# Sample queries and keys projected beside the out-projection of the layer before; turned prompt rows copied by ScalarE and stored, with value rows, from ScalarE's queue

## The chip, the cores and the metric

The kernel runs on one core of one Trainium2 chip. The metric is the device time of one execution in microseconds; the time given for a kernel is the median of its runs.

## What is computed

One inference step of four layers over 1024 prompt rows and 32 sample rows (8 sequences of 4 tokens), width 1024, fp32. Layers 0 and 3 mix with a gated short convolution, layer 1 with a gated linear recurrence (RG-LRU), layer 2 with differential attention. A layer modulates its input, mixes, projects out, adds the residual and normalises. What the change touches is the end of layer 1 and the start of layer 2:

```python
xp = layer_norm(DEEPNORM_ALPHA * xp + gtp * op, ln_g[i], ln_b[i])   # op = mixer output @ w_out
xs = layer_norm(DEEPNORM_ALPHA * xs + gts * osm, ln_g[i], ln_b[i])
...
q, k, v, z = jnp.split(u @ w_in, [QK_WIDTH, 2 * QK_WIDTH, 2 * QK_WIDTH + V_WIDTH], axis=-1)
q = rope_partial(q.reshape(bsz, t, 2 * N_HEADS, HEAD_DIM), pos) * (HEAD_DIM ** -0.5)
k = rope_partial(k.reshape(bsz, t, 2 * N_HEADS, HEAD_DIM), pos)
...
s_past = jnp.einsum('bqhd,bkhd->bhqk', q, k_past)     # sample queries against 2048 cached keys
```

Prompt queries attend to prompt keys; sample queries attend to 16 cached pages per sequence, found through a page table, and to their own new keys. Rotated keys and values of both groups are also outputs.

## The kernel before, in words

Prompt and sample columns stand side by side: 1056 columns in three chunks of 384, 384 and 288, the last holding 256 prompt and the 32 sample columns. Every large product is made of three fp32r products (high and low parts), so one 128-row output block of one chunk takes 24 instructions of TensorE (`gemm_chunk`, line 120).

**Between layers** `boundary` (line 1618) runs `out_proj` (line 264): chunk by chunk, 8 output blocks each. In the first chunk the eight weights are loaded (`ld`, through two `raw` slots of 512 KB and a split by ScalarE and DVE). For each block it loads a residual tile xr from SP's queue (two buffers), multiplies, and adds on DVE (line 287). After a chunk, `norm` turns it (rt), normalises, and `modulate` (line 227) turns it back (xt) and writes the next layer's input units, `us` holding the sample columns for layer 2 (line 260). The chunks run in the order 0, 1, 2.

**Layer 2** starts with `qkv` (line 985): the weights stand in six column groups n of 512 (two each of q, k, v), each loaded in four parts through the same two `raw` slots and split (lines 1003, 1004). `prompt_tile` (line 1053) makes 128 prompt rows of one group: 24 products (line 1060), a scaled copy by ScalarE (1064), for q and k a rotation on DVE (1016 to 1027), four transposes into a single PSUM bank (1073), a copy of it by DVE (qkfs, 1075), and a store to qd or kd from SP's queue (1076). Value rows are stored from SP too (1069, 1085). The sample rows of groups 0 to 3 are made in tiles 1 to 4 of group 0: the four weight parts of a group are fetched again unsplit (`fetch(..., "s")`), `sample_half` (1007) multiplies with column tiling (four 32-column strips of the array), and `sample_rows` (1031) copies, sums the strips with a selection matrix `sel`, rotates and transposes into qsb and ksb. Those of groups 4 and 5 use the weights when they pass for the prompt.

**Beside** `qkv` and the gate projection `zpath` runs the key stream of the samples, `sample_keys`: pages of 256 KB fetched from GpSimd's queue (1354) into a ring of six, turned by DVE (1444), multiplied in bursts (1388), then softmax and turning. It needs qsb and ksb. `attn_layer` (line 1529) weaves the two: `merge` hands out side steps in proportion to the main work's cost, and three prompt tiles run before the first side step. When the gate projection and the key stream are emitted, `heads` (line 1138) starts: it loads keys (twice, into raw slots, then split), values V and queries of a head, and runs 64 blocks of causal attention, with the sample values (128 pages of 512 KB on SP's queue) woven in.

The order on each engine's queue is fixed when the program is built: a scheduler simulates the emitted instructions and orders them by simulated time, with tile buffers and pool memory reused through waits. At run time each queue is in order.

## Time and profile before

| | us |
|---|---|
| median of 3 runs | 2441.85 (2439.98 to 2446.5) |
| profiled execution, its own time | 2443.42 |
| its span | 2441.8 |
| TensorE busy in the span | 2297.3 (94%) |
| DVE busy | 1469.6 (60%) |
| ScalarE busy | 910.1 (37%) |
| DMA, mean rate over the span | 161 GB/s |

The profile is one execution; PE stands for TensorE, PEld for its weight load, ACT for ScalarE, POOL for GpSimd, SP for the queue of SyncE that issues most DMAs. Times in views are counted from the span's start. The out-projection of layer 1 lies at 817 to 925 us, the projections of layer 2 with the key stream at 925 to 1507 us, the heads at 1507 to 1880 us. A wait is put down to what came last; PEclk is the granted share of TensorE's full clock.

### The profile page before, as it was taken

What the parts mean: (1) busy time and instruction counts of PE and PEld (TensorE: products, weight loads), DVE (VectorE), ACT (ScalarE), POOL (GpSimd) and SP (SyncE); (2) the same over time, 40 slices, a digit from 0 to 9 for tenths busy, and PEclk for the clock granted to TensorE, in tenths of its full rate; (3) what the DMA queues carried; (4) which work ended last, traced back from release to release, by engine and by line L of the source; (5) the groups of instructions that cost most, each with busy time, mean ns of one, the idle gap of its engine ahead of it and who ended that gap; (6) DMA issues with size and microseconds to landing.
All of it is one profiled execution on the core that took longest, in us unless ns stands there. A gap on an engine that the chain in (4) does not pass through costs nothing.

```text
span 2441.8 us, 45387 instructions
## 1 busy us (share of the span) xinstructions
PE 2297.3 (94%) x17288; PEld 1952.8 (80%) x17288; DVE 1469.6 (60%) x3047; ACT 910.1 (37%) x1874; POOL 341.7 (14%) x541
## 2 busy tenths in 40 slices
PE   7999999999999998998989997889898999999997
PEld 4989999997888995466656786555566999999997
DVE  5866665467555555555654553676676477666655
ACT  4333333245555233111111111666665254333410
POOL 0200000001010001222223222333321000000000
PEclk9999999999999998999999998999999999999999
DMA  9243335334344425656768765999992321222442
GB/s 327 80 141 105 96 113 164 119 97 124 119 138 130 147 83 185 211 180 211 234 200 271 235 216 170 294 283 293 294 320 87 100 93 53 70 62 71 123 132 75
DMA packets 289392, 393.42 MB, mean 161 GB/s; under 512 B 18749, under 2 KB 197054, under 8 KB 289174
## 3 DMA queue, kind: packets, MB, share of 16 engines
q1 hardware_dynamic: 268694, 323.40, 43.3%
q0 software_dynamic: 20480, 67.13, 8.8%
q8 instruction: 136, 2.23, 0.4%
q14 instruction: 82, 0.67, 0.1%
HBM read 331.14 MB, written 59.31 MB: 160 GB/s over the span
## 4 chain that ended last, share of the span: by engine, by line
PE 67%; issue 13%; DMA 10%; POOLq 4%; DVE 2%; POOL 2%; ACT 1%; SPq 1%; DVEq 0%; ACTq 0%
PE op L127 15%; PE inX L605 12%; PE inZ L605 6%; DMA vp<-cache_v 4%; PE xb L127 4%; PE z L127 4%; PE in L127 3%; POOLq L1347 3%; PE inY L605 3%; PE ada L195 3%; DMA tok<-qd 2%; PE in L726 2%; PE in L641 2%; PE qk L1060 2%; PE zz L127 2%
## 5 line engine op out<-in xcount | busy, mean ns | idle before, releaser
L1060 PE MATMUL qk<-wq,ua 128*128 128x512 f32 x1152 | 289.6, 408 | 2.5 <-DVE wq L1004 2.5
L1060 PEld LDWEIGHTS qk<-wq,ua 128*128 128x128 f32 x1152 | 218.8, 193 | 72.1 <-issue 18.2
L1444 DVE STREAM_TRANSPOSE kt<-kp 128x512 f32<-128x512 f32 x256 | 171.3, 696 | 127.4 <-DMA kp<-cache_k 95.1
L1354 POOL DMA_DIRECT2D kp<-cache_k x256 | 140.4, 548 | 391.8 <-DVE kt L1444 262.5
L1177 PE MATMUL S<-ks,qhl 128*128 128x512 f32 (+2 forms) x384 | 109.9, 396 | 24.5 <-issue 12.3
L1229 ACT ACTIVATE P<-S,rr 128x512 f32<-128x512 f32 (+2 forms) x192 | 110.5, 581 | 49.7 <-DVE rr L1217 26.7
L287 DVE SCALAR_TENSOR_TENSOR r<-op,gate,xr 128x384 f32<-128x384 f32 (+1 forms) x96 | 54.3, 570 | 116.8 <-PE op L127 79.6
L1177 PEld LDWEIGHTS S<-ks,qhl 128*128 128x128 f32 x384 | 61.3, 198 | 60.1 <-ACT P L1229 24.6
L1492 PE MATMUL sacc<-vp,pv 128*16 128x256 f32 x1024 | 81.2, 395 | 24.1 <-DMA vp<-cache_v 23.8
L127 PEld LDWEIGHTS z<-ub,wrz 128*128 128x128 f32 x576 | 92.6, 188 | 11.7 <-issue 10.1
L127 PE MATMUL z<-ub,wrz 128*128 128x384 f32 (+1 forms) x576 | 98.2, 326 | 0.0
L1064 ACT ACTIVATE qkr<-qk 128x512 f32<-128x512 f32 x48 | 28.4, 594 | 186.1 <-PE qk L1060 146.9
L127 PEld LDWEIGHTS zz<-ua,wz 128*128 128x128 f32 x576 | 93.6, 190 | 3.6 <-issue 3.4
L127 PE MATMUL zz<-ua,wz 128*128 128x384 f32 (+1 forms) x576 | 96.1, 326 | 0.0
L1270 PEld LDWEIGHTS pv<-V,wt 128*128 128x128 f32 x576 | 75.8, 198 | 23.0 <-ACT wt L1262 11.6
L127 PEld LDWEIGHTS xb<-ub,wrx 128*128 128x128 f32 x504 | 80.9, 188 | 12.7 <-issue 9.2
L1388 PE MATMUL sps<-kt,qbd 32*32 32x512 f32 x2048 | 86.2, 625 | 4.1 <-DVE kt L1444 2.7
L1270 PE MATMUL pv<-V,wt 128*128 128x128 f32 x576 | 84.5, 289 | 4.3 <-ACT wt L1262 3.6
L324 POOL TENSOR_TENSOR rs<-mv,mhalf 128x1 f32<-128x1 f32 (+1 forms) x36 | 19.2, 540 | 494.5 <-DVE mv L322 489.0
L127 PE MATMUL xb<-ub,wrx 128*128 128x384 f32 (+1 forms) x504 | 87.8, 328 | 0.0
L195 PE MATMUL ada<-wada,ct 128*32 128x512 f32 x384 | 82.5, 616 | 4.3 <-DMA wada<-w_ada 3.1
L127 PE MATMUL op<-ub,ua 128*128 128x384 f32 (+1 forms) x504 | 85.5, 326 | 0.0
(488 smaller groups left out, 5176.0 us busy)
## 6 DMA issues: line engine op xcount, KB each, us to landing
kp<-cache_k POOLq DMA_DIRECT2D x256, 256.0 KB, 3.7
vp<-cache_v SPq DMA_DIRECT2D x128, 512.0 KB, 10.0
wada<-w_ada SPq DMA_DIRECT2D x96, 512.0 KB, 4.2
xa<-xat SPq DMA_DIRECT2D x64, 192.0 KB, 2.2
wra<-a_w_in SPq DMA_DIRECT2D x24, 512.0 KB, 4.1
wrb<-a_w_in SPq DMA_DIRECT2D x24, 512.0 KB, 4.1
xr<-xa SPq DMA_DIRECT2D x64, 192.0 KB, 2.5
tok<-kd SPq DMA_DIRECT2D x32, 256.0 KB, 9.6
```

Source lines behind the costliest of these rows:

```text
L127: nc.tensor.matmul(ps[:, :n], wt[:, wp, k], self.ucols(units[k], up, c), start=i == 0, stop=i == 3 * KB - 1)
L195: nc.tensor.matmul(ps[c : c + 32, :], self.ct[:, k], wts[k // 2][:, k % 2], start=k < 4, stop=k >= 4, tile_position=(0, c),)
L605: nc.tensor.matmul(B[tgt][jj][:, :QH], w[n][:, wp, k], mov[k](jj, up), start=new and m == 0, stop=m == 11, skip_group_check=not new)
L1060: nc.tensor.matmul(ps, u[k][:, c0 : c0 + 128], wq[n, k // 2][:, wp, k % 2], start=i == 0, stop=i == 3 * KB - 1)
L1177: nc.tensor.matmul(st[:, o : o + w], qs[h, g][:, part, s, 128 * qj : 128 * qj + 128], ks[h][:, s, l0 : l0 + w], start=part == 0, stop=part ...
L1229: nc.scalar.activation(p[:, o : o + w], x["S"][s][i][:, :w], AF.Exp, scale=-1.0, bias=rr[:, 6 + s : 7 + s], accum_out=rr[:, c : c + 1])
L1270: nc.tensor.matmul(x["pv"], x["w"][kb // 4][:, j : j + 128], V[h][:, kb], start=kb == 0, stop=kb == qb)
L1347: ld, (r,) = nc.values_load_multi_w_load_instructions(self.ptab[0:1, idx : idx + 1], engines=[et], min_val=0, max_val=159)
L1354: d = eng.dma_start(t, a[src].rearrange(pat)[bass.ds(r, 1), :, cs].rearrange("a p f -> p (a f)"))
L1388: nc.tensor.matmul(ps[b][32 * g : 32 * g + 32, r], qf[rows, f, g, k], kt[rows, g, k], start=f == 0 and k == 0, stop=f == 1 and k == 3, til ...
L1444: nc.vector.transpose(ktv[:, :, j], ring.pop(0).rearrange("p (f t) -> p f t", t=32))
L1492: nc.tensor.matmul(acc[32 * g : 32 * g + 16, :], pt[:k, j, g], vv[:k, :, g], start=j == 0, stop=j == NPG, tile_position=(0, 32 * g))
```

## The change

The sample rows of q and k (groups 0 to 3) are made in `boundary` of layer 1, by a generator `sample_qk`, one step of which is taken before each of the 16 blocks of the second and third chunk. A step fetches one weight part of 512 KB, one step ahead, and multiplies the part before it (two k blocks). The result is summed over the strips, rotated and transposed as before, with one PSUM bank ("acc", the bank Q) for both products; `out_proj` keeps three banks where it had four, and the turned tiles xat have four buffers where they had six. As the sample columns are needed early, the chunk order of that out-projection becomes 2, 0, 1, and group 0 of `qkv` starts with tiles 6 and 7. The selection matrix is made in `setup`, the rotation table and qsb, ksb stand in a pool opened before the boundary.

In `prompt_tile` ScalarE copies the turned rows (fs) and issues their store and the two stores of value rows; the store of rotated keys to the output stays on SP. The key stream is woven in after one prompt tile instead of three. `heads` loads its first keys, values and queries when 20 of the 24 steps of the gate projection are emitted, from a pool of its own; before, this came after the key stream.

`rope` becomes a method `rotate`, and `sample_rows` keeps only the value groups.

```diff
@@ -156,6 +156,11 @@
         self.mhalf = cp.tile([128, KB * NQ], F32, name="mhalf")
         nc.gpsimd.memset(self.mhalf, -0.5)
         self.us = cp.tile([128, KB, S], F32, name="us")
+
+        self.sel = cp.tile([128, 128], F32, name="sel")
+        for g in range(4):
+            nc.vector.tensor_reduce(
+                self.sel[:, 32 * g : 32 * g + 32], self.ident.rearrange("p (g j) -> p j g", g=4), axis=AX.X, op=ALU.add)
...
-    def out_proj(self, l, wout, yu, wu):
+    def out_proj(self, l, wout, yu, wu, order, hook):
...
-        for c in range(3):
+        for ci, c in enumerate(order):
             c0, n = CH[c]
             npr = min(n, T - c0)
             rt = []
             for d in range(KB):
-                if c == 0 and d + 1 < KB:
+                if ci == 0 and d + 1 < KB:
                     ld(d + 1)
+                if ci > 0:
+                    next(hook, None)
...
-                if c == 2 and d == 7:
+                if ci == 2 and d == 7:
                     yield c, rt, False
...
-            ps.append(self.half(l, c, i, rt, 1, self.mm if c == 2 and i >= 1 else self.tp))
+            ps.append(self.half(l, c, i, rt, 1, self.mm if first and i >= 1 else self.tp))
...
+    def sample_qk(self):
+        nc, a = self.nc, self.a
+        wv = a["d_w_in"][0].rearrange("(k p) f -> p k f", p=128)
+        todo = [(n, j) for n in range(4) for j in range(4)]
+        raws = []
+
+        def fetch():
+            if todo:
+                n, j = todo.pop(0)
+                raws.append(self.raw([128, 2, 512], f"wq{n}_{j}s"))
+                nc.sync.dma_start(raws[-1], wv[:, 2 * j : 2 * j + 2, 512 * n : 512 * n + 512])
+
+        def rows(n, pr):
+            kind, m = "qk"[n // 2], n % 2
+            ps = self.bank("acc", f"qss{n}")
+            nc.tensor.matmul(ps, self.sel, pr, start=True, stop=True)
+            rt = self.tmp.tile([128, 512], F32, tag="sr", bufs=1, name=f"qsr{n}")
+            nc.scalar.mul(rt, ps, -0.125 if kind == "q" else 1.0)
+            self.rotate(rt, 128, 8, self.tmp, 2)
+            if kind == "k":
+                nc.sync.dma_start(
+                    a["k_sample"][0, :, :, 8 * m : 8 * m + 8, :].rearrange("b t s f -> (b t) (s f)"), rt[:S]
+                )
+            dst = self.qsb if kind == "q" else self.ksb
+            nc.vector.transpose(dst[:, 16 * m : 16 * m + 16].rearrange("p f t -> p (f t)"), rt)
+
+        fetch()
+        done = None
+        for n in range(4):
+            if done:
+                rows(*done)
+            acc = self.bank("acc", f"qs{n}")
+            for j in range(4):
+                fetch()
+                raw = raws.pop(0)
+                for k in (2 * j, 2 * j + 1):
+                    c = 32 * (k % 4)
+                    nc.tensor.matmul(
+                        acc[c : c + 32, :], self.us[:, k], raw[:, k % 2], start=k < 4, stop=k >= 4,
+                        tile_position=(0, c))
+                yield
+            pr = self.tmp.tile([128, 512], F32, tag="spr", bufs=1, name=f"qsp{n}")
+            nc.scalar.copy(pr, acc)
+            done = n, pr
+        rows(*done)
...
         def prompt_tile(n, t):
             kind, m = "qkv"[n // 2], n % 2
...
-                rope(rt, 128, t)
+                self.rotate(rt, 128, t, self.ropep, 4)
             rows = slice(128 * t, 128 * t + 128)
             if kind == "v":
-                nc.sync.dma_start(self.vd[rows, 512 * m : 512 * m + 512], rt)
+                nc.scalar.dma_start(self.vd[rows, 512 * m : 512 * m + 512], rt)
             else:
                 ft = self.tp(f"qkf{n}_{t}")
                 for j in range(4):
                     nc.tensor.transpose(ft[:, 128 * j : 128 * j + 128], rt[:, 128 * j : 128 * j + 128], self.ident)
                 fs = self.pq.tile([128, 512], F32, tag="fs", bufs=3, name=f"qkfs{n}_{t}")
-                nc.vector.tensor_copy(fs, ft)
-                nc.sync.dma_start(
+                nc.scalar.copy(fs, ft)
+                nc.scalar.dma_start(
                     self.qkT["qk".index(kind)][512 * m : 512 * m + 512, rows].rearrange("(j p) t -> p j t", p=128),
                     fs.rearrange("p (j t) -> p j t", j=4),
                 )
@@ -1082,7 +1121,7 @@
                     a["k_prompt"][0, 0, rows, 8 * m : 8 * m + 8, :].rearrange("p s f -> p (s f)"), rt
                 )
             if kind == "v":
-                nc.sync.dma_start(
+                nc.scalar.dma_start(
                     a["v_prompt"][0, 0, rows, 4 * m : 4 * m + 4, :].rearrange("p s f -> p (s f)"), rt
                 )

@@ -1090,18 +1129,12 @@
         for j in range(4):
             load(0, j)
         for n in range(6):
-            for t in range(8):
-                d = t - 2 if n == 0 else t
+            for i in range(8):
+                d = i - 2 if n == 0 else i
                 if n < 5 and d in (0, 1, 3, 4):
                     load(n + 1, (0, 1, None, 2, 3)[d])
-                prompt_tile(n, t)
-                if n == 0 and 1 <= t < 5:
-                    for e in range(2):
-                        fetch(t - 1, 2 * e, "s")
-                        fetch(t - 1, 2 * e + 1, "s")
-                        sample_half(t - 1, e)
-                    sample_rows(t - 1)
-                if n > 3 and t == 0:
+                prompt_tile(n, (6, 7, 0, 1, 2, 3, 4, 5)[i] if n == 0 else i)
+                if n > 3 and i == 0:
...
-                ks[h] = self.pp.tile([128, 2, T], F32R, tag="ks", bufs=self.n_ks, name=f"ks{h}")
-                V[h] = self.pp.tile([128, 8, 128], F32, tag="V", bufs=2, name=f"V{h}")
+                ks[h] = self.ppa.tile([128, 2, T], F32R, tag="ks", bufs=self.n_ks, name=f"ks{h}")
+                V[h] = self.ppa.tile([128, 8, 128], F32, tag="V", bufs=2, name=f"V{h}")
...
+        keys(0, 0)
+        queries(0, 0)
+        keys(0, 1)
+        yield 0

         self.cmask = self.pp.tile([128, 512], F32, name="cmask")
         nc.gpsimd.memset(self.cmask[:, :384], 0.0)
         nc.sync.dma_start(self.cmask[:, 384:], self.a["cmask"])
-        keys(0, 0)
-        keys(0, 1)
-        queries(0, 0)
...
-        for _ in range(3):
-            next(g)
-        merge(g, 45 * 5120.0, keys, self.shares[0] * KEY_COST)
+        next(g)
+        merge(g, 47 * 5120.0, keys, self.shares[0] * KEY_COST)
         cq.__exit__(None, None, None)
         ct, self.tmp = self.pool("tmpq", reuse_waits="tile")
-        merge(self.zpath(u), 8 * 10.2 * NT, keys, self.shares[1] * KEY_COST)
+        z, ztot = self.zpath(u), 8 * 10.2 * NT
+        merge(itertools.islice(z, 20), ztot, keys, self.shares[1] * KEY_COST)
+
+        cpa, self.ppa = self.pool("ppa", reuse_waits="tile")
+        hs = self.heads(u)
+        next(hs)
+        merge(z, ztot, keys, self.shares[1] * KEY_COST)
         rest(keys)
...
-        def boundary(l, wout, y, u):
+        def boundary(l, wout, y, u, order=(0, 1, 2), hook=iter(())):
             first = None
-            for c, rt, full in self.out_proj(l, wout, y, u):
+            for c, rt, full in self.out_proj(l, wout, y, u, order, hook):
                 if not full:
+                    for _ in hook:
+                        pass
+                    self.deal(tp="PPPQ", mm="RRRU")
...
+            cs, sp = self.pool("smq", side="right")
+            self.rope = sp.tile([128, 2, 9, 16], F32, name="rope")
+            nc.sync.dma_start(self.rope, a["rope"])
+            self.qsb = sp.tile([128, 32, S], F32, name="qsb")
+            self.ksb = sp.tile([128, 32, S], F32, name="ksb")
             ct, self.tmp = self.pool("tmpm", reuse_waits="tile", side="right")
-            boundary(1, a["r_w_out"][0], A, B)
-        cms = [ct, cb]
+            self.bufs = dict(bufs, xat=4)
+            self.deal(tp="PPPU", mm="RRR", acc="Q")
+            boundary(1, a["r_w_out"][0], A, B, (2, 0, 1), self.sample_qk())
...
```

## Rows read from the trace of the kernel before

**Rows 1.** Windows: us, busy us (instructions) of PE, PEld, DVE, ACT, POOL; clock; DMA share; GB/s
```profile
817.00:925.00 108.00, 108.00 (x708) 107.05 (x707) 55.99 (x119) 34.48 (x55) 3.18 (x6) 1.00 0.36 111
925.00:1507.00 582.00, 531.67 (x4658) 385.74 (x4657) 310.63 (x650) 104.23 (x167) 145.53 (x272) 0.95 0.67 212
...
1507.00:1880.00 373.00, 312.88 (x2486) 205.29 (x2484) 250.62 (x657) 241.25 (x733) 113.28 (x80) 0.94 0.92 266
```

**Rows 2.** Waits of PE, 925 to 1510: who, for whom, total us, times, longest
```profile
PE qkf L1073 <- DVE qkfs L1075: 10.2, 5, 4.2
PE qs L1012 <- DMA wq_3s<-d_w_in: 9.6, 3, 3.9
PE spn L1397 <- DVE qkfs L1075: 7.6, 2, 5.6
...
PE qs L1012 <- DMA wq_0s<-d_w_in: 3.8, 1, 3.8
...
PE qk L1060 <- DVE wq L1004: 2.5, 2, 2.2
```

**Rows 3.** Waits of POOL, DVE, ACT and SP's queue, 925 to 1510
```profile
POOL kp L1354 <- DVE kt L1444: 262.5, 126, 27.0
...
DVE kt L1444 <- DMA kp<-cache_k: 95.1, 106, 4.5
...
ACT wq L1003 <- DMA wq_0r<-d_w_in: 37.4, 5, 11.3
...
SPq L1076 <- DVE qkfs L1075: 67.9, 20, 17.8
```

**Rows 4.** Window 925:1106 of L1012 alone (PE, PEld); groups of lines in it
```profile
925.00:1106.00 181.00, 20.24 (x64) 2.42 (x64) 0.92 0.64 200
...
L1036 PE MATMUL qss<-qsp,sel 128*128 128x512 f32 x8 | 5.5, 772 | 0.0
L1034 ACT COPY qsp<-qs 128x512 f32<-128x512 f32 x4 | 2.3, 587 | 22.2 <-PE qs L1012 22.2
```

**Rows 5.** Timeline of PE: start, us, instruction and count
```profile
937.46 1.04 PE L1012 MATMUL qs<-wq_0s,us 128*32 128x512 f32 x2
...
946.07 1.05 PE L1012 MATMUL qs<-wq_1s,us 128*32 128x512 f32 x4
...
1015.84 1.12 PE L1036 MATMUL qss<-qsp,sel 128*128 128x512 f32 x2
```

**Rows 6.** Chain of waits, first chunk of the out-projection: start, us, what
```profile
817.21 33.51 PE op L127 x192
```

**Rows 7.** DMA issues, 925 to 1106: transfer, count, KB each, median us to landing
```profile
wq_0s<-d_w_in SPq DMA_DIRECT2D x4, 512.0 KB, 4.8
...
wq_2s<-d_w_in SPq DMA_DIRECT2D x4, 512.0 KB, 3.7
```

**Rows 8.** Waits of SP's queue, 815 to 930
```profile
SPq L284 <- DVE r L287: 30.4, 10, 10.4
```

**Rows 9.** Timeline of SP's queue
```profile
832.67 0.38 SPq L992 DMA_DIRECT2D wq_0r<-d_w_in  x1
```

**Rows 10.** Lines 1075 and 1076, 925 to 1510: count, duration min/median/max in ns
```profile
L1075 DVE COPY qkfs<-qkf x32: 649/684/693, 965.5 to 1259.5; 128x512 f32<-128x512 f32 x32
...
L1076 SPq DMA_DIRECT2D qd<-qkfs x16: 359/366/462, 966.9 to 1114.6; - x16
```

**Rows 11.** Windows with the lowest clocks, columns as in rows 1
```profile
955.00:1015.00 60.00, 48.67 (x267) 21.93 (x272) 24.16 (x63) 5.84 (x10) 12.26 (x22) 0.82 0.75 241
...
1510.00:1525.00 15.00, 2.71 (x14) 1.58 (x14) 0.52 (x2) 1.05 (x2) 5.51 (x4) 0.56 1.05 281
```

**Rows 12.** Waits of PE, 1500 to 1885
```profile
PE S L1177 <- issue: 12.3, 1, 12.3
```

**Rows 13.** DMA issues, 1106 to 1507
```profile
tok<-kd SPq DMA_DIRECT2D x4, 256.0 KB, 4.2
```

More of the change, by code (lines that the diff above doesn't have):

```diff
@@ L956, in attn_consts @@
         nc, a = self.nc, self.a
-        self.rope = cp.tile([128, 2, 9, 16], F32, name="rope")
-        nc.sync.dma_start(self.rope, a["rope"])
         self.smask = cp.tile([128, NB, S], F32, name="smask")
@@ L974, in attn_consts @@
         )
-        self.sel = cp.tile([128, 128], F32, name="sel")
-        for g in range(4):
-            nc.vector.tensor_reduce(
-                self.sel[:, 32 * g : 32 * g + 32], self.ident.rearrange("p (g j) -> p j g", g=4), axis=AX.X, op=ALU.add)
         self.coef = cp.tile([128, NB], F32, name="coef")
@@ L982, in attn_consts, with rotate @@
         self.ots = cp.tile([128, KB, S], F32, name="ots")
+    def rotate(self, rt, w, t, pool, bufs):
+        nc = self.nc
+        rv = rt[:w].rearrange("p (s f) -> p s f", f=64)
+        x = rv[:, :, 0:16]
+        tt = []
+        for q in range(2):
+            r = pool.tile([128, 8, 16], F32, tag="rp", bufs=bufs, name=f"rp{rt.name}_{q}")
+            nc.vector.tensor_tensor(
+                r[:w], x, self.rope[:w, q, t : t + 1, :].to_broadcast([w, 8, 16]), ALU.mult
+            )
+            tt.append(r)
+        nc.vector.tensor_tensor(rv[:, :, 0:8], tt[0][:w, :, 0:8], tt[1][:w, :, 8:16], ALU.add)
+        nc.vector.tensor_tensor(rv[:, :, 8:16], tt[0][:w, :, 8:16], tt[1][:w, :, 0:8], ALU.add)
@@ L1014, in sample_half @@
                     raws[n, k // 2][:, 0], start=e == 0, stop=e == 1, tile_position=(0, c))
[L1016 to L1027 removed]
         def sample_rows(n):
[L1032 removed]
+            m = n % 2
             pr = self.pq.tile([128, 512], F32, tag="rt", bufs=3, name=f"qsp{n}")
@@ L1037, in sample_rows @@
             rt = self.pq.tile([128, 512], F32, tag="rt", bufs=3, name=f"qsr{n}")
[L1038 to L1051 removed]
+            nc.scalar.copy(rt, ps)
+            nc.sync.dma_start(
+                a["v_sample"][0, :, :, 4 * m : 4 * m + 4, :].rearrange("b t s f -> (b t) (s f)"), rt[:S]
+            )
+            nc.sync.dma_start(self.vsd[:, 512 * m : 512 * m + 512], rt[:S])
         def prompt_tile(n, t):
@@ L1366, in sample_keys @@
         cw, wp = self.pool("psw", space=PSUM, reuse_waits="tile")
-        self.qsb = kp.tile([128, 32, S], F32, name="qsb")
-        self.ksb = kp.tile([128, 32, S], F32, name="ksb")
         qb = kp.tile([128, 2, 4, 2, 2, 32], F32, name="qbd")
@@ L1568, in main @@
         def main():
-            hs = self.heads(u)
             while True:
@@ L1692, in run @@
             self.attn_layer(2, A)
-            for cm in (cr, cc):
+            for cm in (cr, cc, cs):
                 cm.__exit__(None, None, None)
```

31 lines of the change are left out of this document (3 added, 28 removed).

## The prediction

> **What bounds the kernel now.** I read the page first: TensorE is busy for 94% of the span, so a gain has to come from its idle time, its slow clock, or work that disappears. The table of windows says where such time is [rows 1]. The out-projection of layer 1 (817 to 925 us) has TensorE busy 108.00 of 108.00 us at granted clock 1.00. The attention projections with the key stream beside them (925 to 1507 us) have it busy 531.67 of 582 us, so 50.3 us idle, at a clock of 0.95. The heads (1507 to 1880 us) have it idle for 60 us, but there the DMA share is 0.92.
>
> TensorE's waits in the middle stretch name the causes [rows 2]: 9.6 + 3.8 = 13.4 us for weight loads of the sample product, 10.2 + 7.6 = 17.8 us for DVE's copy of turned rows (qkfs), the rest small and scattered. The chain of waits runs through GpSimd's page loads here, but GpSimd itself spends 262.5 us waiting for DVE to free pages [rows 3]: the key stream is paced by others. TensorE, which has least room, is what I count.
>
> **The change, part by part.**
>
> *Sample rows leave the projections.* The four groups for q and k are 64 instructions and 20.2 us of TensorE, their selection products 5.5 us [rows 4]. With the 13.4 us of waits, 20.2 + 5.5 + 13.4 = **39.1 us** leave the stretch.
>
> *They arrive beside the out-projection*, which has no idle time, so they are paid in full. A visit there is one generator step: two k blocks, four instructions. At full clock four take 1.05 us [rows 5]: 16 x 1.05 = 16.8 us. Four selection products at 1.12 us [rows 5] make 4.5 us. Sum **21.3 us**, which is also the lower end: the same instructions at full clock. Where the scheduler splits a visit, two instructions alone take 1.04 us [rows 5]; 32 such visits and the products are 37.8 us, the upper end. I take the lower, as both blocks of a visit come from one load and are ready together.
>
> That row shows that a visit costs the same for two instructions as for four. The Trainium skill, TensorEngine Tiling (Array Packing), section Key Properties, says that changing the tiling mode drains TensorE; each visit changes it twice, inside a stream of uniform products, so the rule speaks against this move. The trace agrees in kind (1.04 us for two against 1.05 us for four). By the rule at its worst, every visit split, the total would come out some 16 us less favourable.
>
> *Loads for them.* Each step fetches 512 KB through two raw slots, one step ahead. A step is 33.51 / 8 = 4.19 us of out-projection [rows 6] plus 1.05 us, so 5.24 us, against a landing of 3.7 to 4.8 us for the same loads [rows 7]. SP issues in order, and in this stretch it waits 30.4 us in ten waits for residual buffers [rows 8]. So most loads should just be hidden, some not: **3 us** of stalls; ends 0 and 13.4, what the same loads cost today.
>
> *The first prompt weights come later.* Before, the first of them is fetched at 832 us, the raw slots being idle [rows 9]. Now the slots are the samples' until the last step, and the first prompt product waits for one or two more loads of about 5 us, partly covered by the transposes of the tail: **4 us**; ends 0 (covered) and 13.4, again the trace's own price for late loads. The new chunk order itself moves equal work. Its last chunk has 384 columns rather than 288, and five prompt tiles that do not need it (6, 7, 0, 1, 2) run beside its normalisation: nothing.
>
> *Copy of turned rows on ScalarE.* Off DVE go 32 x 0.684 = 22 us [rows 10]. ScalarE gets 32 copies at 0.59 us, as its other 128x512 copy from PSUM [rows 4], so 19 us, and 64 DMA issues. The trace has no issue from ScalarE; I take SP's 0.37 us each [rows 10], 24 us. ScalarE is busy 104 of 582 us [rows 1], so it has room for 43 more. The bank that the copy frees is the only one of its kind, and DVE came late because page transposes ahead in its queue wait for pages (95.1 us in all, [rows 3]). Part of that lateness will hit the rotation instead, which stays on DVE behind the same transposes. I take half of 17.8: **-9 us**; ends 0 and -17.8. If ScalarE waits for weights (37.4 us for wq_0 alone, [rows 3]), the copies queued behind that cast wait too, and so do the scaled rows of the next tile: that is the end at 0.
>
> *Stores on ScalarE's queue.* Their data come from ScalarE itself, just before them. On SP such a store held 67.9 us of waiting [rows 3] ahead of weight loads, but TensorE waited for late prompt weights for only 2.5 us [rows 2]: I credit nothing. An issue that ScalarE exposes at 0.37 us, 64 times, would take 24 us at most; as three banks buffer ScalarE's input, I keep 0.
>
> *Clock.* From 955 to 1015 us TensorE is busy 48.67 us at 0.82 [rows 11]: 48.67 x 0.18 = 8.8 us lost. Of that 25.7 - 21.3 = 4.4 us stands already in the sample work. The gaps before it are the sample waits, so the other **-4 us** go; ends 0 and -9, the latter if later dips, behind qkfs waits, go as well.
>
> *Heads' first loads before the key stream ends.* TensorE waits 12.3 us for its first score [rows 12]; from 1510 to 1525 us it is busy 2.71 of 15 us [rows 11]. But the DMA engines are full from there on. What leaves that full stretch is V, 512 KB, and two query loads of 256 KB; the four key loads were early already [rows 13]. At 281 GB/s [rows 11] this 1 MB is 3.7 us. Between 3.7 and 12.3 us: **-8 us**, the middle, since DMA is not full to the end of the heads (share 0.92, [rows 1]) and TensorE can keep part of the head start.
>
> *Rest.* The selection matrix moves to setup, four short reductions on DVE: nothing.
>
> Sum: +21.3 + 3 - 39.1 + 4 - 9 - 4 - 8 = **-31.8 us**. The profiled execution took 2443.42 us, 1.6 above its span and 1.6 above the median of 2441.85; the same difference on the median gives **2410 us**.
>
> **Rivals.**
>
> *Waits only change their cause*: DVE's rotation takes over from qkfs, late prompt weights from late sample weights. For it: DVE waits 95 us for pages, with the rotation in the same queue. Then +21.3 + 3 - 25.7 - 8 = -9.4 us: 2432 us. Chance 0.19.
>
> *ScalarE's casts hold the copies*, so that only the -9 us fails: 2419 us. For it: its wait for wq_0. Against: 32 copies to 24 casts in half a millisecond, most of them apart. Chance 0.15.
>
> *All ends favourable*: +21.3 - 39.1 - 17.8 - 9 - 12.3 = -56.9 us: 2385 us. For it: the rows show little else that TensorE waits for. Against: nothing may go wrong anywhere. Chance 0.10.
>
> *Slower: the out-projection starves on sample loads.* Place: SP, in the 16 steps. If every fetch stands behind a residual load that waits 30.4 / 10 = 3.0 us [rows 8], a load takes 3.0 + 4.8 + 1.05 = 8.9 us against a step of 5.24: 3.6 us of stall in each, 58 us instead of 3: -31.8 + 55 = +23 us, 2465 us. It decides from about 2.2 us of stall per load, 35 us in all. Against: two slots overlap the loads, and the DMA share is only 0.36 there [rows 1]. Chance 0.14.
>
> *The change does not do what it says*: the scheduler puts the sample work after the out-projection, as its input comes from a chunk that has to be normalised first. Then 39.1 us stand in the projections as before and only copy and heads gain, 17 us: 2425 us. Inside the range and counted with the first rival.
>
> **How the numbers follow.** The forecast has the remaining 0.42. The range takes in the three milder rivals and part of the way to the slower one: 2382 to 2446 us, with some 0.15 above and 0.05 below. Faster by over 0.3% (below 2434.5 us; 0.3% is about what a measurement of this kernel can tell from no change) are the forecast and the three milder rivals, less 0.07 for the first one's spread: 0.79. Same 0.07. Slower 0.14.
>
> **What would show it.** Right: sample products at about 1.05 us a visit in an out-projection of some 132 us at clock 1.00; no waits for sample loads in the projections; qkfs waits gone, or half gone under the rotation's name; projections and key stream in some 534 us instead of 582; the first score directly behind the last gate product. Wrong: TensorE waiting over 13 us for sample loads in the out-projection, or over 13 us between it and the first prompt tile; other waits in the projections growing by what these lose; heads no shorter although their first loads are early.

## The result, and the profile after

The changed kernel takes 2405.61 us in the median of 4 runs (2400.01 to 2409.33), the kernel before 2443.71 in the 4 runs beside them; the ratio is 0.984 with a 95% interval of 0.981 to 0.987. The profiled execution, the slowest of the four, took 2409.33 us for a span of 2407.7, against 2443.42 and 2441.8 before: 34.1 us less. All times of stretches below are from profiled executions.

Windows of the changed kernel, cut where TensorE passes from one kind of work to the next: out-projection of layer 1, last sample visits, projections with the key stream, heads, layer 2's out-projection to the end. Columns as in [rows 1].

```profile
816.70:942.00 125.30, 123.17 (x738) 106.65 (x735) 54.29 (x143) 33.82 (x58) 4.61 (x14) 0.99 0.49 148
942.00:947.30 5.30, 5.30 (x31) 2.60 (x29) 3.43 (x6) 0.89 (x2) 0.00 (x0) 1.00 0.45 117
947.30:1486.20 538.90, 499.91 (x4621) 383.08 (x4620) 290.20 (x584) 125.61 (x198) 151.39 (x271) 0.97 0.71 220
1486.20:1848.30 362.10, 304.65 (x2467) 200.14 (x2466) 253.89 (x660) 240.03 (x732) 102.87 (x73) 0.97 0.93 268
1848.30:2407.70 559.40, 544.94 (x4014) 541.23 (x4014) 347.72 (x636) 178.14 (x313) 20.96 (x57) 0.99 0.29 87
```

The same cuts in the kernel before, which fall at other times than the round ones of [rows 1]:

```profile
817.20:920.30 103.10, 103.10 (x675) 102.78 (x674) 51.13 (x111) 33.68 (x55) 3.18 (x6) 1.00 0.37 115
920.30:1509.60 589.30, 538.92 (x4709) 392.13 (x4706) 315.83 (x657) 106.67 (x170) 147.03 (x274) 0.95 0.66 210
1509.60:1882.20 372.60, 310.37 (x2467) 203.03 (x2467) 251.34 (x658) 241.07 (x734) 111.78 (x79) 0.93 0.92 265
1882.20:2441.80 559.60, 545.12 (x4016) 541.46 (x4016) 348.97 (x638) 178.15 (x313) 20.93 (x57) 0.99 0.29 88
```

Four differences make the 34.1 us. The out-projection grew by 22.2 us (103.1 to 125.3; 22.0 counted from its first product, as in the table below). The projections shrank by 45.1 (589.3 to 5.3 + 538.9). The heads shrank by 10.5. The rest and the start differ by 0.2 and 0.5.

Inside the projections the 45 us can be split once more, into three parts. Idle time: 589.3 - 538.9 = 50.4 us before, 544.2 - 505.2 = 39.0 after, so 11.4 less. Time lost to the clock: 538.9 x 0.05 = 26.9 before, 505.2 x 0.03 = 15.2 after, so 11.7 less. What is left, 22 us, I put down to work at full clock that is no longer there. As the clock is shown to a hundredth, the last two are known to some 5 us only.

TensorE's waits in that stretch of the changed kernel (950 to 1490 us: who, for whom, total us, times, longest), to be held against [rows 2]:

```profile
PE sps L1420 <- DVE kt L1476: 11.9, 4, 6.6
PE zz L127 <- DVE zt L1165: 7.0, 3, 5.4
PE qk L1099 <- DVE wq L1067: 5.5, 6, 1.7
...
PE qkf L1112 <- DVE qkr L996: 4.0, 3, 2.4
```

The sample loads (13.4 us) and the copies qkfs (17.8 us) are gone from the list altogether. In their place stand waits that were small before: for transposed pages (sps, 11.9 for 2.7), for DVE's last step on a gate product (zt), which frees the bank for the next one (zz, 7.0 for none), for cast weights (5.5 for 2.5). DVE itself waits for pages a little longer than in [rows 3], 107.1 us for 95.1, and GpSimd, which asks for them, much less for DVE, 188.8 us for 262.5:

```profile
DVE kt L1476 <- DMA kp<-cache_k: 107.1, 117, 7.4
...
POOL kp L1388 <- DVE kt L1476: 188.8, 116, 16.2
```

The sample visits, from the first to the last (window 860:948, line 1038 and then line 1016 alone: PE, PEld, clock, DMA share, GB/s), for [rows 4]:

```profile
860.00:948.00 88.00, 14.76 (x64) 2.04 (x64) 1.00 0.51 155
860.00:948.00 88.00, 4.08 (x8) 1.39 (x8) 1.00 0.51 155
```

That is 14.8 us of visits and 4.1 of selection products, where [rows 4] has 20.2 and 5.5. The timeline of TensorE shows three kinds of visit (start, us, instruction, count; in brackets idle time and what ended it), for [rows 5], and then the first prompt product:

```profile
876.87 1.05 PE L1038 MATMUL qs<-wq_1s,us 128*32 128x512 f32 x4
877.86 4.27 PE L127 MATMUL op<-ua,ub 128*128 128x384 f32 x23
882.05 1.05 PE L1038 MATMUL qs<-wq_2s,us 128*32 128x512 f32 x4
...
894.14 0.62 PE L1038 MATMUL qs<-wq_0s,us 128*32 128x512 f32 x2
894.16 0.62 PE L1038 MATMUL qs<-wq_1s,us 128*32 128x512 f32 x2
894.60 0.60 PE L1038 MATMUL qs<-wq_0s,us 128*32 128x512 f32 x2
894.61 0.60 PE L1038 MATMUL qs<-wq_1s,us 128*32 128x512 f32 x2
...
920.94 1.04 PE L1038 MATMUL qs<-wq_2s,us 128*32 128x512 f32 x2
...
948.09 0.73 PE L1099 MATMUL qk<-wq,ua 128*128 128x512 f32 x2 [0.77 <-ACT wq L1066]
```

There are 14 visits, not 16: three have eight instructions, nine have four, two have two. Twelve lie in the out-projection; the last two and the last selection products lie just behind its end, among the transposes of its tail:

```profile
942.05 1.05 PE L1038 MATMUL qs<-wq_2s,us 128*32 128x512 f32 x4
943.03 0.87 PE L315 MATMUL rt<-ident,r 128*128 128x128 f32 x6
943.84 1.05 PE L1038 MATMUL qs<-wq_3s,us 128*32 128x512 f32 x4
...
946.29 1.02 PE L1016 MATMUL qss<-qsp,sel 128*128 128x512 f32 x2
```

TensorE's one wait in the out-projection, where [rows 1] has none, is not for a sample load but for DVE's first residual add (r), and the clock falls behind it (waits from 816 to 948 us, and a window):

```profile
PE rt L315 <- DVE r L294: 2.1, 1, 2.1
```

```profile
828.00:834.00 6.00, 5.37 (x29) 5.36 (x30) 3.66 (x8) 1.65 (x3) 0.00 (x0) 0.72 0.71 216
```

The first score, with the idle time of [rows 12] gone; it comes ahead of the last gate products:

```profile
1482.75 0.40 PE L1210 MATMUL S<-ks,qhl 128*128 128x256 f32 x2
1482.99 3.20 PE L127 MATMUL zz<-ua,wz 128*128 128x288 f32 x23
```

### The profile page after: what moved, and what is told of

It is laid out like the page before. It is cut to its first block, busy times and chain, and to the rows that moved or that the text cites. A ratio compares the mean times of both kernels' runs of the same rounds, so it can differ in the third digit from the quotient of the medians.

```text
span 2407.7 us, 45325 instructions
## 1 busy us (share of the span) xinstructions
PE 2277.3 (95%) x17288; PEld 1946.8 (81%) x17288; DVE 1453.2 (60%) x3015; ACT 929.2 (39%) x1906; POOL 337.1 (14%) x541
## 4 chain that ended last, share of the span: by engine, by line
PE 64%; issue 13%; DMA 11%; POOLq 5%; POOL 2%; DVE 2%; ACT 1%; SPq 1%; DVEq 0%; ACTq 0%
PE op L127 15%; PE inX L612 12%; PE inZ L612 6%; DMA vp<-cache_v 6%; PE xb L127 4%; PE z L127 4%; POOLq L1381 4%; PE in L127 3%; PE inY L612 3%; PE ada L200 3%; PE in L733 2%; PE in L648 2%; PE g L903 2%; POOL kp L1388 2%; PE sacc L1524 1%
## 5 line engine op out<-in xcount | busy, mean ns | idle before, releaser
L1099 PE MATMUL qk<-wq,ua 128*128 128x512 f32 x1152 | 284.1, 401 | 8.7 <-DVE wq L1067 5.5
L1099 PEld LDWEIGHTS qk<-wq,ua 128*128 128x128 f32 x1152 | 213.2, 189 | 68.4 <-DVE wq L1067 8.1
L1476 DVE STREAM_TRANSPOSE kt<-kp 128x512 f32<-128x512 f32 x256 | 172.0, 697 | 138.5 <-DMA kp<-cache_k 107.1
L1388 POOL DMA_DIRECT2D kp<-cache_k x256 | 137.9, 539 | 336.1 <-DVE kt L1476 188.8
L127 PEld LDWEIGHTS zz<-ua,wz 128*128 128x128 f32 x576 | 95.6, 193 | 11.4 <-DVE zt L1165 7.8
L127 PEld LDWEIGHTS z<-ub,wrz 128*128 128x128 f32 x576 | 92.6, 188 | 11.7 <-issue 10.1
L1303 PEld LDWEIGHTS pv<-V,wt 128*128 128x128 f32 x576 | 73.7, 194 | 22.5 <-ACT wt L1295 13.4
L1420 PE MATMUL sps<-kt,qbd 32*32 32x512 f32 x2048 | 78.8, 621 | 11.9 <-DVE kt L1476 11.9
L127 PE MATMUL op<-ua,ub 128*128 128x384 f32 (+1 forms) x504 | 89.7, 333 | 0.0
L127 PEld LDWEIGHTS op<-ua,ub 128*128 128x128 f32 x504 | 81.9, 192 | 9.1 <-issue 9.0
```

The source lines that it names most:

```text
L127: nc.tensor.matmul(ps[:, :n], wt[:, wp, k], self.ucols(units[k], up, c), start=i == 0, stop=i == 3 * KB - 1)
L1099: nc.tensor.matmul(ps, u[k][:, c0 : c0 + 128], wq[n, k // 2][:, wp, k % 2], start=i == 0, stop=i == 3 * KB - 1)
L1303: nc.tensor.matmul(x["pv"], x["w"][kb // 4][:, j : j + 128], V[h][:, kb], start=kb == 0, stop=kb == qb)
L1388: d = eng.dma_start(t, a[src].rearrange(pat)[bass.ds(r, 1), :, cs].rearrange("a p f -> p (a f)"))
L1420: nc.tensor.matmul(ps[b][32 * g : 32 * g + 32, r], qf[rows, f, g, k], kt[rows, g, k], start=f == 0 and k == 0, stop=f == 1 and k == 3, til ...
L1476: nc.vector.transpose(ktv[:, :, j], ring.pop(0).rearrange("p (f t) -> p f t", t=32))
```

## The experiments

Twelve kernels ran. The table gives the median of each, its ratio to the kernel before, run beside it, with the 95% interval, and four stretches of the profiled execution: out-projection (O), projections to the last gate product (P), heads to the second out-projection (H), the rest (R).

| kernel | us | ratio | O | P | H | R |
|---|---|---|---|---|---|---|
| before | 2443.71 | 1 | 103.3 | 589.2 | 372.6 | 559.7 |
| after | 2405.61 | 0.984 (0.981-0.987) | 125.3 | 544.2 | 362.1 | 559.4 |
| b_samples | 2422.52 | 0.993 (0.990-0.995) | 125.9 | 553.5 | 358.1 | 559.6 |
| b_samples_only | 2427.30 | 0.994 (0.992-0.996) | 124.7 | 546.3 | 375.0 | 558.7 |
| b_copy | 2439.27 | 0.998 (0.996-1.000) | 103.3 | 574.6 | 371.3 | 558.8 |
| a_copy_dve | 2414.19 | 0.989 (0.985-0.992) | 125.3 | 553.9 | 354.6 | 558.5 |
| a_no_heads | 2406.19 | 0.985 (0.981-0.990) | 125.5 | 539.8 | 362.1 | 559.6 |
| a_heads_old | 2416.61 | 0.989 (0.985-0.993) | 126.1 | 539.6 | 377.0 | 559.4 |
| a_stores_sp | 2406.19 | 0.985 (0.981-0.989) | 125.3 | 541.6 | 357.5 | 559.7 |
| x_eight | 2404.25 | 0.985 (0.981-0.989) | 119.7 | 536.6 | 368.1 | 560.4 |
| p_split | 2427.5 (one run) | | 148.9 | 541.6 | 358.1 | 560.0 |
| p_no_loads | 2393.57 | 0.981 (0.976-0.985) | 126.9 | 526.0 | 361.5 | 560.0 |
| x_ring7 | 2395.39 | 0.980 (0.976-0.985) | 125.5 | 534.3 | 358.5 | 559.6 |
| x_eight_ring7 | 2396.27 | 0.981 (0.977-0.985) | 119.8 | 536.2 | 362.1 | 559.3 |

P and H of kernels with the same heads differ by several us from one execution to the next, so a single part is judged by the medians, and a stretch only where its difference is larger than that.

**b_samples: the sample rows' move without the other parts.** After, with the copies and stores as before, and the heads' generator started behind the key stream:

```diff
-                nc.scalar.copy(fs, ft)
-                nc.scalar.dma_start(
+                nc.vector.tensor_copy(fs, ft)
+                nc.sync.dma_start(
...
-        z, ztot = self.zpath(u), 8 * 10.2 * NT
-        merge(itertools.islice(z, 20), ztot, keys, self.shares[1] * KEY_COST)
-
+        merge(self.zpath(u), 8 * 10.2 * NT, keys, self.shares[1] * KEY_COST)
+        rest(keys)
         cpa, self.ppa = self.pool("ppa", reuse_waits="tile")
         hs = self.heads(u)
         next(hs)
-        merge(z, ztot, keys, self.shares[1] * KEY_COST)
-        rest(keys)
```

> The kernel before with the move of the sample rows alone: sample queries and keys beside the out-projection in chunk order 2, 0, 1, prompt tiles 6 and 7 first, key stream after one prompt tile; the copy of turned rows on DVE, all stores on SP and the heads' first loads after the key stream, as before. My theory, from the terms of the prediction: +21.3 + 3 - 39.1 + 4 - 4 = -14.8 us against the kernel before, so about 2429 us. Rival (waits only change their cause): the moved work alone, +21.3 + 3 - 25.7 = -1.4 us, about 2442 us.

Measured: -18 us by the ratio. But the heads were short here too (358.1 us), so this was not the move alone: it keeps the new order keys, queries, keys ahead of the sample values' loads, and the gain of the heads goes with it (a_no_heads, below). The clean version is b_samples_only.

**b_copy: the copies and stores alone,** on the kernel before:

```diff
-                nc.vector.tensor_copy(fs, ft)
-                nc.sync.dma_start(
+                nc.scalar.copy(fs, ft)
+                nc.scalar.dma_start(
```

(and the two stores of value rows likewise.)

> The kernel before with only the copy of turned rows on ScalarE and the stores of turned and value rows from its queue. My theory: -9 us, half of the 17.8 us of qkfs waits, so about 2435 us, with waits under the rotation's name grown. Rival 1 (ScalarE's weight casts hold the copies): 0, about 2443 us. Rival 2 (the wait is gone for good): -18 us, about 2426 us.

Measured: -4 us by the ratio, with an interval from -9 to +1, so not clear of nothing. TensorE's waits in its profiled execution (920 to 1500 us; at 2426.64 us the fastest of ten) show where the rest stayed:

```profile
PE qkf L1073 <- DVE qkr L1027: 10.1, 5, 4.1
...
PE spn L1397 <- ACT qkfs L1075: 3.3, 1, 3.3
...
PE qkf L1073 <- ACT qkfs L1075: 1.4, 1, 1.4
```

Of the 17.8 us behind qkfs 4.7 are left; but the wait for the rotation on DVE, one step earlier in the same chain, grew from 2.8 to 10.1 us. Of the 13.1 us that went, 7.3 only changed their name.

**a_copy_dve: the copies and stores undone in the changed kernel** (the first hunk of b_samples alone).

> The changed kernel with the copy of turned rows back on DVE and the stores back on SP. My theory: about +9 us against the changed kernel, 2415 us. Rival (in the changed kernel other waits grew by as much as the qkfs waits fell, so nothing was won by the copy there): within 2 us of the changed kernel, 2404 to 2408 us. If the gain was whole: +18 us, 2424 us.

Measured: 8.6 us slower than after. Waits for qkfs are back (942 to 1500 us), and one put down to sc, another instruction of DVE's queue:

```profile
PE qkf L1112 <- DVE sc L1436: 6.6, 1, 6.6
PE qkf L1112 <- DVE qkfs L1114: 6.4, 5, 2.3
```

So the copies are worth 4 us alone and 8.6 on top of the rest; the intervals overlap, and whether the two differ stays open.

**a_no_heads: the heads' first loads issued behind the key stream's code** (the second hunk of b_samples alone).

> The changed kernel with the heads' first loads after the key stream again (one memory pool for keys and values kept). My theory: the first score waits again some 12 us behind the last gate product, and about 8 to 10 us come back, 2414 to 2416 us. Rival (the heads are bound by DMA, so only the 1 MB that was moved counts): +3.7 us, about 2409 us.

Measured: 2406.19 us, nothing lost. TensorE's first score still comes ahead of the last gate product. The place in the code is not the cause: loads are placed by the planner when their tiles come free, and what the edit left alone is the order of the first loads, ahead of the mask and the sample values, and the pool of their own for keys and values.

**a_heads_old: the heads wholly as before** (keys, keys, queries behind the mask, generator started with the sample values, keys and values in the heads' common pool again):

```diff
-        keys(0, 0)
-        queries(0, 0)
-        keys(0, 1)
-        yield 0
...
         nc.sync.dma_start(self.cmask[:, 384:], self.a["cmask"])
+        keys(0, 0)
+        keys(0, 1)
+        queries(0, 0)
...
+            hs = self.heads(u)
             while True:
```

> The changed kernel with the heads' start wholly as in the kernel before: first loads emitted after the key stream and behind the sample values' first loads, both key halves ahead of the queries, one pool. The run a_no_heads kept the new order of these loads (keys, queries, keys) and their place ahead of the sample values and lost nothing. My theory now: it is this order, not the point in the gate projection, that lets the first score start at once; so here the wait of about 12 us is back and 8 to 10 us come back, 2414 to 2416 us. Rival (DMA-bound heads): +3.7 us, about 2409 us.

Measured: 11 us slower than after. The wait of [rows 12] is back at its old size, and H is 377.0 us:

```profile
PE S L1210 <- issue: 12.2, 1, 12.2
```

So the heads' part is worth 11 us. The first loads of queries go out at 1484.97 and 1485.81 us here, behind the mask's, and land at 1493.60, just before the first score at 1494.83; in after the first goes out at 1443.28, in a_no_heads at 1439.47. What lets them go early, the order of the loads, their place ahead of the mask and the sample values, or the pool of their own for keys and values, was not tried apart.

**b_samples_only: the sample rows' move with nothing else** (a_heads_old with the copies undone).

> The kernel before with the move of the sample rows alone, the heads' start wholly as before (the run b_samples carried the new order of the heads' first loads with it). My theory: -14.8 us by the terms of the prediction, about 2430 us. Rival (waits only change their cause): the work alone, about -1 us, 2443 us. If the whole of b_samples' gain was the move: -18 us, 2426 us.

Measured: -15 us by the ratio (2442 x 0.0063). O grew by 21.4 us as in after, P shrank by 42.9. The three parts alone make 15 + 4 + 11 = 30 us of the 38 between the medians; with the copies at their 8.6 they make 35.

**p_split: visits cut in two.** Each step's two weight blocks are visited apart, half a chunk between them, held there by order edges (the residual load is also emitted ahead of the visit):

```diff
                 ps = self.gemm_chunk(wts[d], yu, c, f"op{l}_{c}_{d}")
+                if ci > 0:
+                    next(hook, None)
...
+                    if k % 2:
+                        self.after(mm, self.mid)
+                    else:
+                        self.qsk = mm
+                    yield
```

> The changed kernel with the same sample product in about 32 visits of two instructions, held apart on TensorE's queue by products of the out-projection. If a visit has one price (0.97 us for two instructions, as for four): some 18 visits more than in the changed kernel, +17 us, out-projection about 143 us, total about 2423 us. If the price goes with instructions: out-projection 125 us, total 2406 us.

Measured: 28 visits instead of 14, 27 of them in the out-projection instead of 12, and an out-projection of 148.9 us, 23.6 more. In the timeline a visit of two lasts as long as one of four did:

```profile
866.95 1.05 PE L1046 MATMUL qs<-wq_0s,us 128*32 128x512 f32 x2
```

Idle time in that stretch grew from 2.1 to 5.1 us (148.90 - 143.81 in the window below). Without these 3.0, 15 more visits cost 20.6 us, 1.4 us each, or 1.3 if the clock of 0.98 for 0.99 is taken off: more than the 1.05 of the visit itself.

```profile
817.20:966.10 148.90, 143.81 (x756) 109.44 (x754) 56.78 (x146) 34.08 (x58) 5.11 (x14) 0.98 0.42 127
```

**x_eight: visits joined,** two weight parts and eight instructions in each, in a set order:

```diff
+            for e in range(2):
+                pair = [raws.pop(0), raws.pop(0)]
+                for k in (4 * e + 2, 4 * e + 3, 4 * e, 4 * e + 1):
...
+                    if last is not None:
+                        self.after(mm, last)
+                    last = mm
                 fetch()
...
+                fetch()
+                yield
                 yield
```

> The changed kernel with the sample product in eight visits instead of some fourteen: two weight parts at a time, four k blocks in four strips, bound together on TensorE's queue. In the changed kernel's timeline eight instructions on four strips take 0.99 us, as four on two strips do, or two on one. My theory (a visit has one price, whatever it holds): six visits fewer, -6 us, out-projection about 119 us instead of 125, about 2400 us. Rival 1 (the price goes with instructions): no change, 2406 us. Rival 2 (two loads that must both have landed starve the out-projection): idle TensorE there, slower than the changed kernel.

Measured: eight visits, seven of them in the out-projection where after has twelve, and O 5.6 us shorter: 1.1 us a visit. A visit of eight instructions lasts about as long as one of four or two, as strips of 32 columns run side by side: two start within 0.01 us of each other (the second half of the visit follows as at 894.60 above).

```profile
878.28 0.62 PE L1039 MATMUL qs<-wq_1s,us 128*32 128x512 f32 x2
878.29 0.62 PE L1039 MATMUL qs<-wq_0s,us 128*32 128x512 f32 x2
...
945.43 1.22 PE L1106 MATMUL qk<-wq,ua 128*128 128x512 f32 x2 [2.97 <-ACT wq L1073]
```

The total moved by 1.4 us, within the intervals. Part went at once: the raw slots are held in pairs, so the first prompt weights come later and the first prompt product waits 2.97 us for them, where it waited 0.77. H was 6 us longer in this execution, which I can't attribute.

**a_stores_sp: the copies stay on ScalarE, the stores go back to SP's queue.**

```diff
                 nc.scalar.copy(fs, ft)
-                nc.scalar.dma_start(
+                nc.sync.dma_start(
```

> The changed kernel with the stores of turned rows and of value rows back on SP's queue, the copy staying on ScalarE. The run a_copy_dve (copy and stores undone) lost some 9 us; this tells which of the two it was. My theory, as in the prediction: the stores earn nothing, 2404 to 2408 us. Rival: it was the stores that stood ahead of weight and page-free loads on SP, so most of the 9 us are lost here, 2412 to 2415 us, with TensorE's waits for weights (5.5 + 1.6 us in the changed kernel) grown.

Measured: 2406.19 us against 2405.61. What the queue of the stores earns or costs is too small for these runs to tell.

**p_no_loads: 15 of the 16 sample weight loads left out.** One loaded part serves every step, so the sample rows of q and k come from wrong weights:

```diff
+        one = self.raw([128, 2, 512], "wq0_0s")
+        nc.sync.dma_start(one, wv[:, 0:2, 0:512])
...
-                raws.append(self.raw([128, 2, 512], f"wq{n}_{j}s"))
-                nc.sync.dma_start(raws[-1], wv[:, 2 * j : 2 * j + 2, 512 * n : 512 * n + 512])
+                raws.append(one)
```

> The changed kernel with one sample weight part loaded and used in all 16 steps; it leaves out the other 15 loads, so the sample rows of q and k come from wrong weights. It prices the loads. My theory: nothing inside the out-projection (no wait for them shows there), and a few us behind it, where the first prompt weights waited for raw slots (3.6 us of short waits from 947 to 959 us): 2400 to 2403 us. Rival: the loads cost little even there, as one raw slot stays occupied here: 2406 us. Were the starving rival of the prediction at work, the out-projection would shrink by 10 us or more.

Measured: the out-projection is not shorter without the loads (126.9 us for 125.3), so they are hidden there in full; it holds twelve visits here too. The total is 12 us shorter, and the gain lies behind it, in P (526.0 for 544.2). Its first 18 us, of p_no_loads and then of after:

```profile
943.60:961.60 18.00, 16.79 (x85) 13.04 (x84) 12.46 (x26) 9.18 (x13) 2.64 (x5) 1.00 0.52 150
```

```profile
942.00:960.00 18.00, 14.28 (x66) 7.89 (x65) 11.48 (x25) 8.32 (x11) 2.61 (x5) 1.00 0.56 154
```

85 instructions for 66, of which 10 are sample work; here no sample visit is left over (3.1 us), and TensorE is idle for 1.2 us where it is for 3.7 in after. That is some 5 us. The remaining gain is spread over the stretch and is not settled.

**x_ring7: one more page buffer for the key stream.** SBUF had no room for it, so the copies of turned rows give up one of three:

```diff
-                fs = self.pq.tile([128, 512], F32, tag="fs", bufs=3, name=f"qkfs{n}_{t}")
+                fs = self.pq.tile([128, 512], F32, tag="fs", bufs=2, name=f"qkfs{n}_{t}")
...
-                ring.append(self.page("cache_k", b * NPG + j, f"kp{b}_{f}_{j}", 6, f))
+                ring.append(self.page("cache_k", b * NPG + j, f"kp{b}_{f}_{j}", 7, f))
...
-        for _ in range(5):
+        for _ in range(6):
```

> The changed kernel with seven page buffers instead of six and six pages fetched ahead instead of five (the buffer taken from the three of the turned rows' copies). In the changed kernel TensorE waits 11.9 us for page transposes, which wait 107 us for pages. My theory: the pages come late because GpSimd issues a fetch only when a transpose has freed a buffer, so one more buffer takes some of it, 2 to 6 us: 2400 to 2404 us. Rival: lateness is set by the rate of landing, or two copy buffers are too few: no gain or a loss, 2406 us or more.

Measured: 2395.39 us, some 10 below after (the intervals of the two ratios overlap a little; so do the runs, 2392.32 to 2401.28 against 2400.01 to 2409.33). DVE's transposes of pages (groups of lines, 900 to 1600 us: busy, mean ns, idle time before them and its causes) wait 92.0 us for pages instead of 107.1:

```profile
L1476 DVE STREAM_TRANSPOSE kt<-kp 128x512 f32<-128x512 f32 x256 | 169.3, 693 | 126.3 <-DMA kp<-cache_k 92.0 <-PE sps L1420 33.8
```

TensorE waits 8.2 us for these transposes instead of 11.9. By its median it is the fastest of the kernels that leave nothing out, ahead of both before and after. That it wins is borne out by the next kernel; that it wins by these waits is not, as the next kernel shows too.

**x_eight_ring7: both.**

> Both edits, eight visits and seven page buffers. If they add: 1.5 us from the first, 2 to 6 us from the second, 2398 to 2402 us, faster than both kernels. Rival: the scheduler's new order moves TensorE's waits elsewhere, 2404 us or more.

Measured: 2396.27 us, the same as x_ring7. The 5.7 us that the out-projection saves (119.8 for 125.5) are lost again behind it, in P and H. Against x_eight it is 8 us faster, and no run of either reaches the other's (2393.23 to 2398.44 against 2402.47 to 2405.71). But TensorE's waits for page transposes went the other way, in x_eight and then here (945 to 1490 us):

```profile
PE sps L1427 <- DVE kt L1483: 8.2, 5, 4.1
```

```profile
PE sps L1427 <- DVE kt L1483: 12.3, 4, 5.8
```

DVE waits 99.0 us for pages in x_eight and 97.7 here. So the edit of x_ring7 is worth 8 to 10 us, but how it earns them, by the page buffer or by what else moved when a copy buffer was given up, is not shown.

## Why the prediction was right, and where its steps were not

The total came out at 2405.61 us for 2410. By parts:

**Sample rows in the out-projection** (+21.3, and 3 of stalls): right in size, and that by luck. O grew by 22.0 us, and the two visits and the selection products behind it take 1.05 + 1.05 + 1.02 = 3.1: 25.1 us for 24.3. But it is made up otherwise. TensorE never waits for a sample load, and p_no_loads is no shorter in O. This also puts out the rival in which the out-projection starves (a load behind each residual wait). SP does wait there, in eight waits and 21.3 us where [rows 8] has ten and 30.4, but two slots cover it:

```profile
SPq L291 <- DVE r L294: 21.3, 8, 9.7
```

In place of these stalls stands the wait for the first residual add at 828 us: 2.1 us, and some 1.5 us more as TensorE then runs 5.37 us at a clock of 0.72, together 3.6. All kernels with the moved sample rows have this wait (2.0 to 3.1 us), before and b_copy have none. I had put the new chunk order at nothing, and the bank that the move takes from the out-projection was in no term. The first blocks now have 288 columns and take less time each, and DVE's first add waits 3.2 us for its residual tile; whether the order or the three banks for four bring the wait was not tried.

The visits cost more than their own time. Fourteen at 1.05 us and four selection products at 1.02 make 18.8 us; with the 3.6 that is 22.4, and 25.1 were paid: 0.15 us more for each of the 18. The row for the 23 products between two visits agrees: they take 4.27 us, 4.19 to the start of the next visit, and 23 of the 192 in 33.51 us [rows 6] would take 4.01, so some 0.2 us. By x_eight and p_split a visit more or less costs 1.1 to 1.4 us in all. My term left out this price of coming and going; fewer visits made up for it.

TensorEngine Tiling (Array Packing), section Key Properties, of the Trainium skill says that a change of tiling mode drains TensorE. The additional 0.2 us in the products before a visit agree with it; no run here separates the drain from other causes. The equal length of visits with two and four instructions, which I took for a sign of it, is none: the strips run side by side.

**Sample work and its waits leave the projections** (-39.1): right. The waits for sample loads, 13.4 us, are gone from the list, and the work with them.

**First prompt weights later** (+4): right. TensorE's gaps between 946 and 959 us sum up to 3.6 us; the first load of prompt weights is issued at 943.14 us, where [rows 9] has it at 832.67:

```profile
943.14 0.37 SPq L1055 DMA_DIRECT2D wq_0r<-d_w_in  x1
```

**Copies on ScalarE** (-9, half of 17.8): right by the -8.6 on top of the rest; alone they gave -4, which is not clear of nothing. The mechanism is the one I gave, and b_copy shows it best: the qkfs waits go, and a part returns as the rotation's. ScalarE's casts do not hold the copies: TensorE waits 4.7 us for the copies in b_copy and not at all in after, so that rival is out. A copy takes 0.586 us on ScalarE, for 0.684 on DVE [rows 10].

**Stores on ScalarE's queue** (0): right as far as a_stores_sp can tell. An issue takes as long there as on SP [rows 10]:

```profile
L1114 ACT COPY qkfs<-qkf x32: 572/586/589, 985.0 to 1238.6; 128x512 f32<-128x512 f32 x32
...
L1115 ACTq DMA_DIRECT2D qd<-qkfs x16: 366/366/393, 985.6 to 1094.3; - x16
```

**Clock and idle time of the projections together**: the clock paid more than I took, and the waits less. By the split above the clock gave 11.7 us where I had 4 + 4.4 = 8.4; the idle time fell by 11.4 where I had 13.4 + 9 - 4 = 18.4. The stretch as a whole shrank by just what my terms make, 39.1 + 9 + 4 - 4 = 48.1 us: it is 45.0 shorter and holds 3.1 of sample work that I had put into the out-projection. But idle time gave 7.0 us too little, and clock and work together 7 too much; that the two meet is luck. The rival "waits only change their cause" was therefore half true: 31.2 us of waits went, and about 20 came.

What came is mostly the key stream's. GpSimd asks for its first page 38.7 us behind the out-projection's end, as before (38.6), and from there the stream's scores come faster: TensorE's bursts of them begin at 1007.18 us and the last at 1463.80, 456.6 us later, where before they spread over 498.0 us (989.35 to 1487.38). As I read it, with less work of TensorE beside it the stream is held less by TensorE and DVE and more by the pages themselves; the two rows of GpSimd and DVE above fit this: its wait for DVE fell by 74 us, DVE's wait for pages rose by 12. Before, TensorE stood at such points behind sample loads and copies; now some of them show the page behind. No run here shows this cause by itself. The longest is the first one, after the first burst:

```profile
1034.23 1.91 PE L1420 MATMUL sps<-kt,qbd 32*32 32x512 f32 x2 [6.64 <-DVE kt L1476]
```

There, and not at 955 to 1015 us as in [rows 11], is now the deepest dip of the clock in the projections, 0.66 in a stretch in which TensorE was busy 10.77 of 15 us:

```profile
1030.00:1045.00 15.00, 10.77 (x142) 4.97 (x143) 5.86 (x15) 1.67 (x3) 3.76 (x7) 0.66 0.53 161
```

The step that failed is in my first part: I read GpSimd's 262.5 us of waiting for DVE as a stream that is paced by others, and did not ask what it would do once they gave way. x_ring7 asks for pages earlier and wins some 10 us, which would fit, but its waits do not show that it wins them there. DVE's step on the gate product (zt, 7.0 us) is the other wait that came; its cause was not tried.

**Heads' first loads** (-8): 10.5 us in the profile and 11 by a_heads_old, inside my ends of 3.7 and 12.3. The first score stands where I said. Two steps of the reasoning stand differently: it is not the code's place that makes the loads early (a_no_heads), and more than 1 MB leaves the full stretch: 268 GB/s x 362.1 us is 97.0 MB, 265 x 372.6 is 98.7, so about 1.7 MB, or 6 us at the 281 GB/s of [rows 11]. And the 12.3 us are not all gone: a wait of 5.9 us stands right behind the first scores. TensorE's next score needs a bank that DVE's last gate step (zt) frees; this step stands in DVE's queue behind the first masking, which waits 7.3 us for the mask:

```profile
PE S L1210 <- DVE zt L1165: 5.9, 1, 5.9
```

```profile
DVE S L1250 <- DMA cmask<-cmask: 7.3, 1, 7.3
```

The mask's load is issued at 1487.19 us, behind the first keys and queries, and lands at 1491.0. Over the whole stretch idle time fell by only 4.8 us (62.2 to 57.5), and TensorE's busy time for as many instructions by 5.7, at a clock of 0.97 for 0.93. An earlier mask was not tried.

**The slower and the other rivals.** The scheduler put sample work behind the out-projection only in part: two visits of 14. All favourable (2385) failed on the new waits.

## What to carry to other kernels

Work that is moved into a stretch without idle time is paid there in full, so move it only with the waits it causes: here 21.4 us were paid for 42.9 us. Count a visit of another shape by the visit, not by its instructions; but fewer visits shorten the stretch that holds them (5.6 us by x_eight), and the total only if nothing behind it is late (1.4 us, within the intervals). When waits vanish, look for what is late next in the same chain and in the stream beside it: here the rotation, the page and the mask. One more page buffer won 8 to 10 us, by a way that is still open.

## What the runs showed of the hardware

Two, four or eight 128 x 32 instructions of 512 columns amid 128 x 128 products take the same 1.04 to 1.07 us, as strips of 32 columns run side by side: two that start 0.01 us apart take 0.62 us each. A visit costs some 0.2 us more in the products around it: 4.19 us from the first of 23 to the next visit, against 4.01.

An issue of a DMA takes 0.366 us on ScalarE's queue as on SP's, and 64 of them moved from one to the other changed the time by 0.6 us, which is nothing that these runs can tell.
